# Two blocks of a model on one core: the tiles that are loaded as stationary operands get start addresses that are multiples of 128 bytes

## The chip, the core and the metric

The kernel runs on one core of a Trainium2 chip. The time is device microseconds of one execution, the median of several. TensorE does the matrix products: for each one it first loads a stationary operand (the "weights" of the array, an instruction of its own, LDWEIGHTS) and then streams a moving operand past it (MATMUL). In the rows below, `d<-ws,h` is a matmul that writes the PSUM tile `d` from the moving tile `ws` and the stationary tile `h`: the last name is the stationary one.

## The reference, cut to what matters

Two blocks follow each other on 2048 tokens of width 1024, all in float32.

```python
# first block
p = rmsnorm(x) @ w_in                       # pool mixer, 4 differential heads, 4 stick-breaking heads
x = x + concat(pool, diff_attention, stick_breaking) @ w_out
x = x + (silu(rmsnorm(x) @ w_gate) * (rmsnorm(x) @ w_up)) @ w_down      # width 2816
x = rmsnorm(x)
# second block
proj = modulated_rmsnorm(x) @ w_in_2        # 7 parts of 512: gated spatial branch and retention branch
y = concat(gmlp_branch, retention_branch) @ w_out_2
out = x + gate * rmsnorm(y)
```

## The kernel before

Tokens go through in four blocks of 512. Every large product is exact to float32 by splitting both operands into a high and a low part (`float32r`, one pass each): `mm3` issues three matmuls for each 128 rows of the contraction, hi*hi, hi*lo and lo*hi, at lines 149, 150 and 151. `dense_T` takes the model's weights `ws` as stationary operand and streams the activations; `dense_N` takes a 128x128 piece of the activations as stationary operand and streams 512 columns of `ws`.

Phase 1 runs the projection of a block (activations `h`) beside the attention of the block before (queries `q` stationary with keys `k` moving at line 557; for the stick-breaking heads values `v` stationary with `pT` moving at line 709; for the differential heads `pT` stationary), and then the output projections (activations `h`, and in the last one the first four of the eight 128-row pieces in tiles `s`). Phase 2 is the feed-forward: gate and up products by `dense_T` (`d` and `u`), then the down product by `dense_N` with stationary tiles `a`. Phase 3 is the second block: seven projections by `dense_N` from `h`, small retention products, and the output projection by `dense_N` with stationary tiles `y`.

The order in which each engine gets its instructions is made at build time by a scheduler that models the engines; nothing is reordered between engines on the chip but by semaphores. Tiles lie in pools, one after another in each partition; a tile starts where the one before ends, at the next multiple of 32 bytes. Pools with narrow tiles (tables of 4, 8 or 16 numbers) therefore push the pools that follow them off the multiples of 128.

The built program gives these places to the stationary operands of nearly all matmuls (bytes past a multiple of 128, in the kernel before and after the change; a piece of a tile is always a multiple of 512 bytes from the tile's start), with the number of their matmuls:

```
stationary      moving (before, now)   matmuls                        before  now
h               ws (0, 0)              3744 of 512, 384 of 256 cols        0    0
ws              h (0, 0)               5568 of 512                         0    0
a               ws (0, 0)              2112 of 512                        32    0
y               ws (0, 0)               768 of 512                        96    0
q               k (64, 96)              672 of 512, 288 narrower          64    0
v (float32r)    pT (96, 96)             224 of 512, 96 narrower           64    0
s, pieces 0, 1  ws (0, 0)                48 of 512                        32   32
s, pieces 2, 3  ws (0, 0)                48 of 512                         0    0
pT (float32)    v (64, 0)               544 of 128                        96   96
x (transposes)  identity (32, 32)       480 of 128                         0   64
b, tmp          several                 508 of 128                        96   64
wsT             b (96, 64)               16 of 512                         0   64
```

Of the kernel before, what the change touches and what calls it, by code (L numbers as in the profile page):

```python
# [17 lines left out]
P = 128  # L18
# [7 lines left out]
NFF = DFF // P  # L26
EPS = 1e-6
NEG = -1.0e30
LARGEST = 3.0e38
# [5 lines left out]
def constants():  # L35
    """Tables that depend on shapes alone."""
    f = np.float32
    c = {}
    c["ident"] = np.eye(P, dtype=f)
    p = np.arange(P)  # L40
    tri = np.where(p[None, :] <= p[:, None], 0.0, NEG).astype(f)
    mask_le = np.concatenate([np.zeros((P, 384), f), tri], axis=1)
    mask_lt = np.where(p[None, :] < p[:, None], 0.0, NEG).astype(f)
    inv_cnt = np.zeros((P, 2, 16), f)
    inv_w = np.zeros((P, 2), f)
    for ch in range(2):
        for half in range(2):
            w = WINDOWS[2 * ch + half]
            rows = slice(64 * half, 64 * half + 64)
            inv_cnt[rows, ch] = (1.0 / np.minimum(np.arange(16) + 1, w)).astype(f)  # L50
            inv_w[rows, ch] = 1.0 / w
    c["tab1"] = np.concatenate([mask_le, inv_cnt.reshape(P, 32), inv_w, mask_lt], axis=1)
    gam = 1.0 - 2.0 ** (-5.0 - np.arange(RH))
    t = np.zeros((P, RH, P))
    for h in range(RH):
        t[:, h] = np.where(p[None, :] >= p[:, None], gam[h] ** -(p[:, None] + 1.0), 0.0)
    c["ret_mask"] = (t * RD ** -0.5).astype(f)
    c["ret_kdec"] = np.stack([gam[h] ** (P - 1.0 - p) * RD ** -0.5 for h in range(RH)], 1).astype(f)
    c["ret_qdec"] = np.stack([gam[h] ** (p + 1.0) for h in range(RH)], 1).astype(f)
    c["ret_qdec2"] = np.stack([gam[h] ** (2 * (p + 1.0)) for h in range(RH)], 1).astype(f)  # L60
    half = RD // 2
    e = (np.arange(half, dtype=f) / f(half)).astype(f)
    inv_freq = (f(1.0) / np.power(f(10000.0), e).astype(f)).astype(f)
    c["inv_freq"] = np.ascontiguousarray(np.broadcast_to(inv_freq, (P, half)))
    c["gmlp_causal"] = (p[:, None] >= p[None, :]).astype(f)
    return c


def layouts(inputs):
    """Small inputs laid out for the chip: vectors as columns, the four pool matrices as diagonal blocks."""  # L70
    cols = lambda v: v.reshape(-1, P).T
# [25 lines left out]

PROJ_NS, OUT_NS = 107.5e3, 44.4e3       # tensor-engine time of one block's projections


class Body:
# [9 lines left out]
    def t(self, pool, shape, tag, dt=F32, bufs=None):  # L111
        kw = {} if bufs is None else {"bufs": bufs}
        return pool.tile(shape, dt, tag=tag, name=self.nm(tag), **kw)

    def hp(self, kind="e"):
        return self.tc.high_priority(self.pri[kind])

# [1 line left out]
    def split(self, hi, lo, src):  # L119
        """src = hi + lo exactly, both in the single-pass format."""  # L120
        nc = self.nc
# [3 lines left out]
    def wgroup(self, w, k0, nk, c0, ncols):  # L125
        """Weights w[128*k0 : 128*(k0+nk), c0 : c0+ncols], split; get(kc, hl, lo, n)."""
        nc = self.nc
# [17 lines left out]
    def mm3(self, ps, pairs):  # L145
        """ps = sum of products of split operands: hi*hi + hi*lo + lo*hi."""
        n = len(pairs)
# [6 lines left out]
    def dense_T(self, ps, get, c, act):  # L154
        """ps[cols, tokens] = w[:, cols]^T act^T."""
        return self.mm3(ps, [((lambda hl, k=k: get(k, hl, c, P)), (lambda hl, k=k: act[k][:, hl]))
                      for k in range(len(act))])

    def dense_N(self, ps, get, n, act, t):
        """ps[tokens of chunk t, cols] = act w[:, cols]."""  # L160
        return self.mm3(ps, [((lambda hl, k=k: act[k][:, hl, t * P:(t + 1) * P]),
                       (lambda hl, k=k: get(k, hl, 0, n))) for k in range(len(act))])

    def rsqrt_mean(self, ss, n, mul, pool=None):
        """(ss * mul + EPS) ** -0.5 on [P, n]."""
        nc = self.nc
# [15 lines left out]
    def transposed(self, xs, evac, banks, spare=None):  # L182
        """Tiles of act^T (split) for four natural token tiles xs; banks: (PSUM pool, tag) in turn."""
        nc = self.nc
# [21 lines left out]
    def normed(self, src):  # L206
        """Natural tiles of rmsnorm(src) without its gain; src(t) gives a DRAM AP [128, D]."""
        nc = self.nc
# [11 lines left out]
    def normed_first(self, src):  # L220
        """As normed, the tiles one by one and on both engines: nothing else can run yet."""
        nc = self.nc
# [29 lines left out]
    def cols(self, v):  # L252
        """A vector [n] as columns [128, n/128]."""
        return v.rearrange("(k p) -> p k", p=P)

# [1 line left out]
    def run(self):  # L257
        tc, nc, a = self.tc, self.nc, self.a
        with ExitStack() as es:
# [9 lines left out]
            self.raw_bufs, self.ws_bufs = 2, 5  # L269
            # how many steps ahead of their place weights, splits, evacuations and scores are scheduled  # L270
            self.pri = dict(w=100, x=0, e=300, s=20)
# [26 lines left out]

# [1 line left out]
    def phase1(self):  # L300
# [45 lines left out]
    def paced(self, steps):  # L346
        """Emit steps (each yields its tensor-engine ns); the time before each and its last matmul."""
        marks, ns = [], 0.0
# [5 lines left out]
    def spread(self, steps, total, paced):  # L354
        """Emit steps that fill the gaps of the paced ones, held back to an even share of them."""
        marks, ns = paced
# [12 lines left out]
    def attention(self, b):  # L369
        """Scores of a unit are issued one unit ahead of its value products."""  # L370
        units = []
# [17 lines left out]
    def lambda_col(self):  # L389
        """-lambda on every partition."""  # L390
        nc, a = self.nc, self.a
# [156 lines left out]
    def scores(self, q, ks, c, k0, w, extra=False):  # L548
        """[128 queries of chunk c, w keys from k0]: exact in hi and lo parts."""
        nc = self.nc  # L550
# [95 lines left out]
    def head_norm(self, src, width, r1, dst):  # L646
        """Headwise norm (its gain is applied to mix^T) of the query chunks from c0 on, one for each of dst."""
        nc = self.nc
# [18 lines left out]
    def sb_unit(self, b, hh, kb, head):  # L667
        """One stick-breaking head, one block of 512 keys; the blocks are swept from the right."""
        nc = self.nc
# [110 lines left out]

# [1 line left out]
    def phase2(self):  # L782
# [58 lines left out]

# [1 line left out]
    def prepare3(self):  # L843
        """Per-channel vectors, modulation, rotary tables and masked spatial weights."""
        nc, a, c3 = self.nc, self.a, self.c3
# [15 lines left out]
        nc.vector.memset(ones, 1.0)  # L861
        # modulation
        nc.scalar.activation(cc, cc, AF.Silu)
# [28 lines left out]
        nc.vector.scalar_tensor_tensor(out=self.gpre, in0=self.gpre, scalar=1.0, in1=gp, op0=ALU.add, op1=ALU.mult)  # L892
        # masked spatial weights, transposed
        causal = self.const("gmlp_causal", [P, P], a["gmlp_causal"], pool=self.ppool)
# [7 lines left out]
        nc.scalar.activation(self.wsT.rearrange("p g t -> p (g t)"), ps, AF.Copy)  # L902
        # rotary tables
        nt = S // P
        posi = self.const("positions_2", [P, nt], a["positions_2"][0].rearrange("(t p) -> p t", p=P), dt=I32, pool=c3)
        pos = c3.tile([P, nt], F32, name="pos")
        nc.vector.tensor_copy(pos, posi)
        fr = self.const("inv_freq", [P, 64], a["inv_freq"], pool=c3)
        halfpi = c3.tile([P, 1], F32, name="halfpi")
# [32 lines left out]
    def group_stats(self, parts, name):  # L942
        """Mean and variance along each of the four parts: tile [P, 4, 2]."""
        nc = self.nc
# [35 lines left out]
    def second(self, b):  # L980
# [11 lines left out]
        act = []  # L992
        # gated spatial branch
        vn = self.t(self.bpool, [P, 4, NT, P], "b")
# [36 lines left out]
        if b < NB - 1:  # L1031
            xs_next = self.second_in(b + 1)
        # retention branch
        kr = self.t(self.bpool, [P, NT, RH, RD], "b")
# [83 lines left out]
        def use_rg(t, ps):  # L1118
            s_ = self.t(self.tpool, [P, 512], "rg")
            nc.scalar.activation(s_, ps, AF.Silu)  # L1120
            nc.vector.tensor_tensor(out=yy[:, t], in0=yy[:, t], in1=s_, op=ALU.mult)
        # held back, to fill the waits of the last chunks
        project(3072, use_rg, [marks[i] for i in (6, 7, 9, 10)])
        to_act(yy)
        if b < NB - 1:
            self.h_next = drain(self.second_T(xs_next))
        # output projection
        yb = [self.t(self.bpool, [P, 2, D], "b") for _ in range(2)]
# [50 lines left out]
```

## Time and profile before

| | |
|---|---|
| median of 3 runs | 3684.72 us (3682.74 to 3689.01) |
| profiled execution, first to last instruction (span) | 3681.9 us |
| TensorE matmul busy | 3591.9 us, 98% of the span, 17664 records |
| TensorE weight load busy | 2982.3 us, 81% |
| VectorE, ScalarE, GpSimd busy | 54%, 40%, 13% |
| mean granted TensorE clock | 0.995 |

The profile records one execution. Its own time is its span; the median of the runs lies 2.8 us above it, the fastest run 0.8 us. A float32 product that isn't split shows as two matmul records, so there are more records than matmuls in the program. The duration given for a matmul overlaps the next one's; how fast they follow each other is read from their starts.

### The profile page before, as it was taken

Reading aid. Unit: us, or ns where it says so; the run is one execution under the profiler, and the core shown is the slowest. Engines: PE = TensorE matmul, PEld = TensorE weight load, DVE = VectorE, ACT = ScalarE, POOL = GpSimd, SP = SyncE. Lnnn points to the kernel's source line nnn. Section 1 sums busy time; section 2 is a strip of 40 time slices with the busy share of each in tenths; the row PEclk is TensorE's granted clock in tenths of the full one; section 3 lists DMA queues with packets and bytes.
Section 4 is the critical chain, followed back from the end, with each engine's and each line's share of the span. In section 5 each row is a group of like instructions: output and inputs, shape, how many; then the busy total and the mean of one; then the engine's idle time right before and its main releaser. Section 6 shows DMA issues by size and latency. Waiting matters only on the chain. (4 is left out here: it accounts for less than half of the span.)

```text
span 3681.9 us, 46663 instructions
## 1 busy us (share of the span) xinstructions
PE 3591.9 (98%) x17664; PEld 2982.3 (81%) x17664; DVE 1986.9 (54%) x3265; ACT 1489.7 (40%) x2588; POOL 466.0 (13%) x769
## 2 busy tenths in 40 slices
PE   8999999989899999999999999999999999999998
PEld 6888888877788888888888888888888878878887
DVE  4557776899866444453334333433345554655444
ACT  4656666676655332233223222322232332333322
POOL 2343231231001100000000000000001120211101
PEclk9999999999999999999999999999999999999999
DMA  7776655644454554443324333433343252432431
GB/s 242 218 213 186 176 172 158 180 126 149 126 159 146 167 171 137 132 159 113 92 92 151 113 92 97 166 115 92 95 145 105 79 178 87 127 118 77 158 91 63
DMA packets 336065, 503.01 MB, mean 137 GB/s; under 512 B 29152, under 2 KB 198112, under 8 KB 335840
## 3 DMA queue, kind: packets, MB, share of 16 engines
q1 hardware_dynamic: 312336, 426.08, 38.2%
q0 software_dynamic: 23504, 73.95, 5.9%
q8 instruction: 139, 2.28, 0.3%
q14 instruction: 86, 0.70, 0.1%
HBM read 424.70 MB, written 75.24 MB: 136 GB/s over the span
## 5 line engine op out<-in xcount | busy, mean ns | idle before, releaser
L123 DVE TENSOR_TENSOR ws<-raw,ws 128x1024 fp32r<-128x1024 f32 x520 | 636.0, 1225 | 630.2 <-ACT ws L122 625.5
L122 ACT ACTIVATE ws<-raw 128x1024 fp32r<-128x1024 f32 x520 | 551.2, 1062 | 959.1 <-PE d L151 527.7
L149 PE MATMUL d<-ws,h 128*128 128x512 f32 (+1 forms) x1376 | 533.9, 390 | 5.0 <-ACT b L1008 4.5
L150 PE MATMUL d<-ws,h 128*128 128x512 f32 (+1 forms) x1376 | 526.1, 383 | 0.0
L151 PE MATMUL d<-ws,h 128*128 128x512 f32 (+1 forms) x1376 | 525.6, 383 | 0.0
L149 PE MATMUL d<-h,ws 128*128 128x512 f32 x1152 | 453.0, 393 | 4.9 <-DVE st L123 4.7
L150 PE MATMUL d<-h,ws 128*128 128x512 f32 x1152 | 450.7, 391 | 0.0
L151 PE MATMUL d<-h,ws 128*128 128x512 f32 x1152 | 450.4, 391 | 0.0
L149 PEld LDWEIGHTS d<-ws,h 128*128 128x128 f32 x1376 | 260.1, 189 | 53.5 <-ACT b L1008 5.8
L151 PEld LDWEIGHTS d<-ws,h 128*128 128x128 f32 x1376 | 259.8, 189 | 48.7
L150 PEld LDWEIGHTS d<-ws,h 128*128 128x128 f32 x1376 | 260.4, 189 | 46.3 <-issue 1.0
L557 PE MATMUL s<-k,q 128*128 128x512 f32 (+2 forms) x960 | 276.6, 388 | 11.1 <-DVE r L664 2.9
L149 PE MATMUL d<-ws,a 128*128 128x512 f32 x704 | 279.0, 398 | 1.6 <-DVE res L837 1.6
L150 PE MATMUL d<-ws,a 128*128 128x512 f32 x704 | 279.4, 398 | 0.0
L151 PE MATMUL d<-ws,a 128*128 128x512 f32 x704 | 276.2, 394 | 0.0
L151 PE MATMUL u<-h,ws 128*128 128x512 f32 x704 | 274.3, 390 | 0.8 <-DVE ws L123 0.8
L149 PE MATMUL u<-h,ws 128*128 128x512 f32 x704 | 274.1, 389 | 0.3 <-ACT ws L122 0.3
L150 PE MATMUL u<-h,ws 128*128 128x512 f32 x704 | 273.9, 389 | 0.0
L149 PEld LDWEIGHTS d<-h,ws 128*128 128x128 f32 x1152 | 216.8, 188 | 49.5 <-DVE st L123 5.1
L151 PEld LDWEIGHTS d<-h,ws 128*128 128x128 f32 x1152 | 216.6, 188 | 44.9
L150 PEld LDWEIGHTS d<-h,ws 128*128 128x128 f32 x1152 | 216.9, 188 | 43.5
L557 PEld LDWEIGHTS s<-k,q 128*128 128x128 f32 x960 | 165.8, 194 | 37.4 <-DVE s L588 5.4
(237 smaller groups left out, 5545.0 us busy)
## 6 DMA issues: line engine op xcount, KB each, us to landing
raw<-in_w_in_dram SPq DMA_DIRECT2D x192, 512.0 KB, 4.1
raw<-in_w_gate_dram SPq DMA_DIRECT2D x88, 512.0 KB, 3.8
raw<-in_w_up_dram SPq DMA_DIRECT2D x88, 512.0 KB, 3.8
raw<-in_w_down_dram SPq DMA_DIRECT2D x88, 512.0 KB, 3.6
raw<-in_w_out_dram SPq DMA_DIRECT2D x64, 512.0 KB, 3.9
k<-qkd SPq DMA_DIRECT2D x120, 256.0 KB, 4.1
qkd<-st POOLq DMA_DIRECT2D x192, 128.0 KB, 3.4
q<-qkd SPq DMA_DIRECT2D x96, 256.0 KB, 4.8
```

The costliest lines, as they stand in the source:

```text
L122: nc.scalar.activation(hi, src, AF.Copy)
L123: nc.vector.tensor_tensor(out=lo, in0=src, in1=hi.bitcast(F32), op=ALU.subtract)
L149: self.nc.tensor.matmul(ps, st(0), mv(0), start=i == 0, stop=False)
L150: self.nc.tensor.matmul(ps, st(0), mv(1), start=False, stop=False)
L151: self.nc.tensor.matmul(ps, st(1), mv(0), start=False, stop=i == n - 1)
L557: nc.tensor.matmul(ps[:, :w], q[:, hl, c * P:(c + 1) * P], kt[:, o:o + w], start=hl == 0, stop=hl == 1 and not extra)
```

## The change

Tiles with the tags `h`, `ws`, `a`, `y`, `q` and `v` are allocated with `align_bytes=128`. Two small tables that only `prepare3` reads, the positions and the inverse frequencies, move from a pool that lives to the end (`c3`) to the pool of that preparation (`ppool`). Comments and docstrings are gone, so lines shift by up to 3. No instruction is added or removed.

```diff
+STATIONARY = {"h", "ws", "a", "y", "q", "v"}
...
     def t(self, pool, shape, tag, dt=F32, bufs=None):
         kw = {} if bufs is None else {"bufs": bufs}
+        if tag in STATIONARY:
+            kw["align_bytes"] = 128
         return pool.tile(shape, dt, tag=tag, name=self.nm(tag), **kw)
...
-        posi = self.const("positions_2", [P, nt], a["positions_2"][0].rearrange("(t p) -> p t", p=P), dt=I32, pool=c3)
+        posi = self.const("positions_2", [P, nt], a["positions_2"][0].rearrange("(t p) -> p t", p=P), dt=I32, pool=self.ppool)
...
-        fr = self.const("inv_freq", [P, 64], a["inv_freq"], pool=c3)
+        fr = self.const("inv_freq", [P, 64], a["inv_freq"], pool=self.ppool)
```

On TensorE, ScalarE and GpSimd every instruction keeps its place. Three instructions move. On SyncE, which issues the loads, the two tables stood before the change behind the last of the small tables, at the end of phase 1, ahead of the last loads of `x` for the output projection:

```order
L246 DMA c_b_ada_cols<-in_b_ada_dram 128x16x1
L246 DMA c_positions_15579<-in_positions_dram 128x16x1
L246 DMA c_inv_freq<-in_inv_freq_dram 128x64
L775 DMA st_12984<-in_x_dram 128x512
L775 DMA st_13013<-in_x_dram 128x512
```

Now they stand 21 loads later, early in phase 2, between two other loads of the preparation and a load of feed-forward weights (`raw`):

```order
L874 DMA px_15460<-in_w_ada_dram 128x1024
L249 DMA c_gmlp_causal<-in_gmlp_causal_dram 128x128
L249 DMA c_positions_15579<-in_positions_dram 128x16x1
L249 DMA c_inv_freq<-in_inv_freq_dram 128x64
L138 DMA raw_13346<-in_w_up_dram 128x4x256
```

On VectorE the conversion of the positions (CAST) stood between two evacuations of the output projection (`st`):

```order
L202 SCALAR_TENSOR_TENSOR h_13132<-tp_13127,c_gains,h_13132 128x512
L778 TENSOR_TENSOR st_12819<-d_12821,st_12819 128x512
L907 CAST pos<-c_positions_15579 128x16
L778 TENSOR_TENSOR st_12848<-d_12850,st_12848 128x512
L202 SCALAR_TENSOR_TENSOR h_13140<-tp_13135,c_gains,h_13140 128x512
```

Now it stands in phase 2, behind the first product of the modulation (`px`) and ahead of a gate product (`sg`) and the scaling of the next block's tokens (`x`):

```order
L126 TENSOR_TENSOR ws_13343<-raw_13341,ws_13343 128x1024
L876 TENSOR_SCALAR px_15459<-px_15460,c_c_15450 128x1024
L910 CAST pos<-c_positions_15579 128x16
L828 TENSOR_TENSOR sg_13325<-sg_13325,u_13300 128x512
L219 TENSOR_SCALAR x_15147<-x_15147,rs_r_15165 128x1024
```

What moved there is the CAST alone; its neighbours follow each other as before.

## Rows read from the trace of the kernel before

**Rows 1.** Page: busy time of the engines; TensorE's granted clock in 40 slices.
```profile
PE 3591.9 (98%) x17664; PEld 2982.3 (81%) x17664; DVE 1986.9 (54%) x3265; ACT 1489.7 (40%) x2588; POOL 466.0 (13%) x769
...
PEclk9999999999999999999999999999999999999999
```
**Rows 2.** Windows of phases 1, 2 and 3: length, busy time and records by engine.
```profile
0.00:1255.00 1255.00, 1188.72 (x6712) 1009.84 (x6713) 896.88 (x1614) 766.26 (x1641) 295.07 (x537) 0.99 0.57 172
1255.00:2752.00 1497.00, 1494.28 (x6611) 1224.76 (x6610) 592.73 (x651) 433.43 (x532) 20.50 (x35) 1.00 0.40 123
2752.00:3682.00 930.00, 908.92 (x4344) 747.74 (x4342) 497.30 (x1000) 290.05 (x416) 150.43 (x197) 1.00 0.35 110
```
**Rows 3.** Longest waits of TensorE in phase 1: total us, times, longest.
```profile
PE o L709 <- DVE pT L123: 17.3, 24, 1.6
```
**Rows 4.** Longest waits of TensorE in phases 2 and 3.
```profile
PE d L149 <- ACT b L1008: 4.5, 3, 2.0
```
**Rows 5.** Windows from a run's first matmul to the next run's first: a, ws, a, y, h.
```profile
1739.17:1783.96 44.79, 44.79 (x193) 36.04 (x192) 14.94 (x17) 7.95 (x8) 0.00 (x0) 1.00 0.25 73
1783.97:1871.04 87.07, 87.07 (x385) 72.09 (x384) 30.28 (x32) 26.46 (x32) 0.00 (x0) 1.00 0.36 108
1871.06:1915.84 44.78, 44.78 (x193) 36.04 (x192) 14.95 (x17) 7.95 (x8) 0.00 (x0) 1.00 0.23 73
2948.39:2982.08 33.69, 33.69 (x144) 27.06 (x145) 15.21 (x16) 11.41 (x20) 4.66 (x9) 1.00 0.61 193
3447.99:3502.38 54.39, 54.39 (x241) 45.06 (x240) 23.72 (x61) 16.10 (x20) 15.12 (x15) 1.00 0.47 148
```
**Rows 6.** TensorE's groups by line and shape: busy us, mean ns; idle before.
```profile
L150 PE MATMUL d<-ws,a 128*128 128x512 f32 x704 | 279.4, 398 | 0.0
...
L557 PE MATMUL s<-k,q 128*128 128x512 f32 x672 | 214.5, 416 | 5.8 <-ACT s L686 2.8 <-DVE s L588 2.2 <-DVE s L602 0.4
...
L150 PE MATMUL d<-ws,y 128*128 128x512 f32 x256 | 101.1, 395 | 0.0
...
L709 PE MATMUL o<-pT,v 128*128 128x512 f32 x224 | 90.0, 439 | 13.4 <-DVE pT L123 10.6 <-ACT pT L122 2.4
...
L1020 PE MATMUL tp<-c_ident,b 128*128 128x128 f32 x128 | 19.4, 274 | 0.4 <-DVE b L1121 0.4
L190 PE MATMUL pp<-c_ident,x 128*128 128x128 f32 x128 | 19.3, 273 | 0.0
```
**Rows 7.** TensorE's timeline in attention: start us, us, instruction and count.
```profile
702.50 0.62 PE L557 MATMUL s<-k,q 128*128 128x512 f32 x2
702.96 0.39 PE L150 MATMUL d<-h,ws 128*128 128x512 f32 x1
...
718.30 0.63 PE L709 MATMUL o<-pT,v 128*128 128x512 f32 x2
718.77 0.38 PE L716 MATMUL tp<-c_ident,s 128*128 128x128 f32 x2
```
**Rows 8.** TensorE's timeline in the last output projection; three rows left out each time.
```profile
1234.76 0.39 PE L149 MATMUL d<-ws,s 128*128 128x512 f32 x1
...
1235.69 0.40 PE L150 MATMUL d<-ws,s 128*128 128x512 f32 x1
...
1236.85 0.39 PE L151 MATMUL d<-ws,s 128*128 128x512 f32 x1
...
1237.76 0.39 PE L149 MATMUL d<-ws,h 128*128 128x512 f32 x1
```
**Rows 9.** Timelines of VectorE and SyncE around the three moved instructions.
```profile
1242.65 0.17 DVE L907 CAST pos<-c_positions 128x16 f32<-128x16 int32 x1 [5.60 <-DMA c_positions<-in_positions_dram]
...
1287.66 0.33 SPq L246 DMA_DIRECT2D c_gmlp_causal<-in_gmlp_causal_dram  x1
1292.88 0.38 SPq L135 DMA_DIRECT2D raw<-in_w_up_dram  x1
...
1297.84 0.75 DVE L873 TENSOR_SCALAR px<-px,c_c 128x1024 f32<-128x1024 f32 x1 [0.35 <-DMA px<-in_w_ada_dram]
```

## The prediction

> **What bounds the kernel now.** I read the page's head first: TensorE is busy 98% of the span and no other engine over 54%, at the full clock throughout (the 2.4 GHz level) [rows 1]. The windows by phase say where that is not quite so: in phase 1 TensorE's rows leave 66 us of 1255 uncovered, in phase 2 only 3 of 1497, in phase 3 21 of 930 [rows 2]. The waits name no single cause: the longest sum in phase 1 is 17 us, for the split of `pT` on VectorE [rows 3], the longest behind it 4.5 us [rows 4]. So in phase 2 nearly every nanosecond between two matmuls' starts is time of the kernel, in phase 3 most, in phase 1 a good part. The change moves addresses, so the question is whether the distance from start to start of two matmuls depends on the stationary tile's address.
>
> The trace can answer that, since some stationary tiles begin at a multiple of 128 bytes already. I took stretches in which TensorE does one thing without a gap and divided their length by the matmuls that start in them (a window's count is one higher where the tail of the matmul ahead reaches in). All are of 512 columns, with the moving operand at a multiple of 128 [rows 5]:
> - `a` stationary, 32 bytes off: 44.79 / 192 = 233.3 ns, and again 44.78 / 192;
> - `ws` stationary, at a multiple: 87.07 / 384 = 226.7 ns, between those two stretches;
> - `y` stationary, 96 off: 33.69 / 144 = 234.0 ns;
> - `h` stationary, at a multiple: 54.39 / 240 = 226.6 ns.
>
> The last two have the same code and the same moving tiles, so it isn't the form of the product. It could still be where in the memory the tiles lie. The last output projection speaks against it: its tiles `s` lie side by side, the first two pieces 32 off, the other two at a multiple. From 1234.76 to 1235.69 four matmuls start with 32-off pieces, 0.93 us or 232 ns each; from 1236.85 to 1237.76 four with pieces at a multiple, 0.91 us or 227 ns [rows 8]. A difference of 20 ns read at 10 ns is weak by itself, but it falls on the same side as the other four.
>
> **The change, part by part.** Clock and order on TensorE stay.
>
> *`a`, the down product.* 704 matmuls on each of three lines, 2112 [rows 6], each 233.3 - 226.7 = 6.6 ns shorter: 13.9 us, all in phase 2, where TensorE waits for almost nothing. The feed holds: the stretch of 44.79 us has 14.94 us of VectorE and 7.95 us of ScalarE in it [rows 5], so a stretch of 43.5 us has room.
>
> *`y`, the second output projection.* 256 on each line, 768 [rows 6], at 234.0 - 226.6 = 7.4 ns: 5.7 us. The stretch of 144 has 15.21 us of VectorE in 33.69 [rows 5]; covered as well.
>
> *`q` and `v`, attention.* 672 and 224 matmuls of 512 columns [rows 6], and 384 narrower ones by the table of places. Their mean durations of 416 and 439 ns contain waits and don't serve [rows 6]. The timeline gives pairs without one: 702.50 to 702.96 is 230 ns each for `q`, 718.30 to 718.77 is 235 ns each for `v` [rows 7]. Against 226.7 that is 3 to 8 ns. With 5 ns for all 1280 the sum is 6.4 us; TensorE stands idle 66 us in this phase [rows 2], and where it waits for a `pT` the shorter matmul only makes it wait longer. I take 4 us. The lower end is 0; the upper end is 8.3 ns on all 1280, 10.6 us.
>
> *`h` and `ws`* were at multiples and stay there: 0.
>
> *Tiles that shift along.* `x` goes from 0 to 64 as the stationary operand of 480 transposes. Transposes of `x` at 0 have 273 ns, those of `b` at 96 have 274 [rows 6]: 1 ns on 480 is under 0.5 us, I take 0. `wsT` goes from 0 to 64 for 16 matmuls; at 7 ns and two records each that is 0.2 us. `k`, which `q` meets as moving operand, goes from 64 to 96: see the third rival.
>
> *The three moved instructions.* Before, the CAST held VectorE 5.60 us until its load came, with an evacuation behind it [rows 9]; TensorE lost at most the waits of phase 1 there, and I take 0. Now the two loads are issued between 1287.66 and 1292.88, where SyncE issued nothing for 4.9 us [rows 9]. The CAST stands behind the `px` product that ends at 1298.59 [rows 9], 10.6 us after the issue; the split of later weights stands behind it. If the load has come by then the price is 0, and that is what I take; the bound above is the wait it had before, 5.6 us, if all of it reached TensorE.
>
> *Sum.* 13.9 + 5.7 + 4 = 23.6 us less than the profiled 3681.9, so a span near 3658. The median of the runs lay 2.8 us above the span; 3684.7 - 23.6 = 3661.
>
> *A rule that speaks against it.* The trace has 233 to 234 ns off the multiples of 128 and 227 at them [rows 5]. The Trainium skill, "SBUF — State Buffer", section "Specifications (TRN2)", counts in lines of 16 bytes: an access pays when it crosses to a new line. 32, 64 and 96 bytes off are whole lines, so by that page a tile touches as many lines after the change as before and the sum would be 0, at 3684.7. The rows speak against that as the whole story. The same page's section "Operand start alignment" asks only for a multiple of the element's size and says that its runs timed nothing.
>
> **The rivals.**
>
> *1. Nothing comes of it.* The 6 to 7 ns belong to something that goes with the place, not with the multiple (`a` and `y` both lie high in the memory, `h` and `ws` low). Then the down stretch stays at 44.8 us and the time at 3685. For it: two of my three comparisons are between distant tiles. Against it: the neighbours in [rows 8], and 7 ns on both `a` and `y`, which other code fills. 0.04. By the page's lines of 16 bytes it would end here too, and the trace doesn't agree.
>
> *2. More comes of it.* Matmuls of `h` and `ws` mixed with those of `q` and `v` in phase 1 may pay for their neighbours; then the attention's part reaches its upper end or beyond, and the time is 3684.7 - 13.9 - 5.7 - 10.6 = 3654.5 or less. For it: [rows 7] has an `h` product directly behind each pair. Against it: the idle time of that phase. 0.08.
>
> *3. Part is given back by the moving side.* `v` pairs have `pT` 96 off and take 235 ns, `q` pairs have `k` 64 off and take 230 [rows 7]. If it is the moving operand that makes the 5 ns, `k` at 96 gives 672 x 5 = 3.4 us, or 960 x 5 = 4.8 us, back, and `q` and `v` gain nothing: 3684.7 - 13.9 - 5.7 + 4.8 = 3670. Against it: one pair of each is little to build on. 0.08.
>
> *4. Slower.* The CAST is on VectorE's path in order. If the load of the positions comes late in the traffic at the start of phase 2, the splits behind the CAST wait, then the stationary tiles, then TensorE. It decides once TensorE stands longer than the 23.6 us that the matmuls give: with the CAST ready at 1298.59, the load would have to land 10.6 + 23.6 = 34 us after its issue. At 42 us, say, TensorE would stand 31 us and the time would be 3692. The wait it had before, 5.60 us, is far below that [rows 9]. 0.02.
>
> **How the numbers follow.** The forecast has 0.78: 3661 us. The likeliest value is 3655 to 3668; with the unknown of attention (0 to 10.6) and the third rival the range is 3654 to 3671. Under 0.2% (7.4 us) a measurement of this kernel can hardly tell from no change. Forecast, second and third rival all lie beyond it on the fast side: 0.78 + 0.08 + 0.08 = 0.94 faster; 0.04 the same; 0.02 slower.
>
> **What would show it.** The stretch of 192 `a` matmuls should take 43.5 us, that of 144 `y` matmuls 32.6 us, while the 384 of `ws` keep 87.1 us. Phase 2 should shrink by 14 us, phase 3 by 5 to 6, phase 1 by 0 to 10. The durations of `d<-ws,a` and `d<-ws,y` should fall from 395 to 398 ns to those of `h` at its best, and VectorE should not wait at the CAST. I am wrong if `a` stays at 233 ns (the multiple of 128 isn't the cause), if phase 2 shrinks by much less than 14 us while the stretch is at 43.5 (a new wait), or if phase 1 grows.

## The result and the profile after

The changed kernel takes 3727.26 us (median of four runs, 3725.41 to 3731.84) where the kernel before takes 3683.73 us (3681.86 to 3689.01) beside it: a ratio of 1.0119, with an interval of 1.0105 to 1.0134. It is slower by 43.5 us, or 1.2%. The forecast was 3661 us, and faster.

The head of its page: the granted clock is 0.995 as before, and TensorE has as many records; its busy time and the span have grown together, by 46.6 and 43.4 us against [rows 1] and the span of before.

```profile
span 3725.3 us, 46660 instructions
...
PE 3638.5 (98%) x17664; PEld 2988.4 (80%) x17664; DVE 1992.3 (53%) x3265; ACT 1489.3 (40%) x2588; POOL 457.0 (12%) x769
```

The same five stretches as in [rows 5], of `a`, `ws`, `a`, `y` and `h` as stationary operand, in the windows of the changed kernel (start and end, length, then busy time and records of TensorE, its weight loads, VectorE, ScalarE and GpSimd, granted clock, DMA share and GB/s):

```profile
1755.71:1800.49 44.78, 44.78 (x193) 36.04 (x192) 15.04 (x17) 7.94 (x8) 0.00 (x0) 1.00 0.23 74
1800.50:1890.09 89.59, 89.59 (x385) 72.10 (x384) 30.14 (x32) 26.44 (x32) 0.00 (x0) 1.00 0.33 104
1890.10:1934.88 44.78, 44.78 (x193) 36.04 (x192) 15.39 (x17) 7.94 (x8) 0.00 (x0) 1.00 0.22 74
2985.76:3019.44 33.68, 33.68 (x144) 27.10 (x145) 15.20 (x16) 11.14 (x19) 4.65 (x9) 1.00 0.60 196
3487.97:3543.72 55.75, 55.75 (x241) 45.23 (x240) 23.55 (x61) 16.09 (x20) 13.28 (x15) 1.00 0.44 146
```

Divided by their matmuls (192, 384, 192, 144 and 240), these are 233.2, 233.3, 233.2, 233.9 and 232.3 ns. `a` and `y` have gained nothing, though they now lie at multiples of 128. `ws` and `h`, which were to stay as they were, have lost: 87.07 us became 89.59, and 54.39 became 55.75.

Where the time went, in windows whose borders are the first gate or up product and the last down product: first the kernel before, then the changed one.

```profile
0.00:1278.67 1278.67, 1212.39 (x6821) 1029.35 (x6822) 907.24 (x1626) 773.95 (x1650) 297.23 (x541) 0.99 0.57 172
1278.67:2751.46 1472.79, 1470.07 (x6500) 1204.81 (x6498) 582.37 (x639) 425.20 (x524) 18.34 (x31) 1.00 0.39 123
2751.46:3681.90 930.44, 909.46 (x4346) 748.19 (x4344) 497.30 (x1000) 290.59 (x417) 150.43 (x197) 1.00 0.35 110
```
```profile
0.00:1288.09 1288.09, 1223.04 (x6822) 1033.14 (x6822) 908.53 (x1626) 774.22 (x1650) 297.33 (x541) 0.99 0.56 170
1288.09:2785.19 1497.10, 1495.01 (x6500) 1206.22 (x6499) 584.98 (x640) 424.09 (x521) 18.24 (x31) 1.00 0.37 121
2785.19:3725.30 940.11, 920.50 (x4346) 749.07 (x4344) 498.79 (x1000) 290.95 (x418) 141.43 (x197) 1.00 0.34 109
```

Phase 1 is 9.4 us longer, phase 2 24.3, phase 3 9.7. In each it is TensorE's busy time that grew, not what it leaves uncovered (65 us in phase 1 now, 66 before; 2.1 and 2.7 in phase 2; 19.6 and 21.0 in phase 3). Nor is there a new wait. The longest of TensorE's waits behind phase 1 in the changed kernel (engine, line, what ended the wait: total us, times, longest):

```profile
PE d L152 <- DVE res L840: 1.4, 1, 1.4
...
PE d L152 <- DVE b L1143: 3.8, 4, 1.3
```

And the CAST, whose load was the fourth rival, waits 0.20 us. VectorE's timeline around it in the changed kernel, which answers to [rows 9]:

```profile
1306.61 0.75 DVE L876 TENSOR_SCALAR px<-px,c_c 128x1024 f32<-128x1024 f32 x1 [0.48 <-DMA px<-in_w_ada_dram]
1307.56 0.17 DVE L910 CAST pos<-c_positions 128x16 f32<-128x16 int32 x1 [0.20 <-DMA c_positions<-in_positions_dram]
```

So the loss is a few nanoseconds on each of some nine thousand matmuls, with nothing waiting. The mean durations, which overlap, show it less clearly than the starts. On the middle line of `mm3`, `ws` as stationary operand goes from 391 to 396 ns (first the kernel before, then the changed one), `a` from 398 in [rows 6] to 396, and `y` stays at 395.

```profile
L150 PE MATMUL d<-h,ws 128*128 128x512 f32 x1152 | 450.7, 391 | 0.0
```
```profile
L153 PE MATMUL d<-h,ws 128*128 128x512 f32 x1152 | 456.2, 396 | 0.0
...
L153 PE MATMUL d<-ws,a 128*128 128x512 f32 x704 | 277.9, 396 | 0.0
...
L153 PE MATMUL d<-ws,y 128*128 128x512 f32 x256 | 101.1, 395 | 0.0
```

What had moved is told by the places in the built programs, now counted to 256 instead of 128 (bytes past a multiple; the pairs that were equal are marked):

```
stationary / moving   before        after        
ws / h                0 / 0   =     0 / 128
h / ws                0 / 0   =     128 / 0
a / ws                160 / 0       128 / 0
y / ws                224 / 0       128 / 0
q / k                 192 / 192 =   128 / 224
v / pT                192 / 224     0 / 96
```

`h` was at a multiple of 128 before and after, but it moved, from byte 66304 to 66432: the pool of `ws` ahead of it is now an aligned pool, and 128 bytes of slack behind it push everything that follows. In the table ahead of the prediction, which counts to 128, this can't be seen.

### The profile page after: what moved, and what is told of

Read it like the earlier page. It is cut to its first block, busy times and chain, and to the rows that moved or that the text cites. A ratio compares the mean times of both kernels' runs of the same rounds, so it can differ in the third digit from the quotient of the medians.

```text
span 3725.3 us, 46660 instructions
## 1 busy us (share of the span) xinstructions
PE 3638.5 (98%) x17664; PEld 2988.4 (80%) x17664; DVE 1992.3 (53%) x3265; ACT 1489.3 (40%) x2588; POOL 457.0 (12%) x769
## 5 line engine op out<-in xcount | busy, mean ns | idle before, releaser
L152 PE MATMUL d<-h,ws 128*128 128x512 f32 x1152 | 458.4, 398 | 4.4 <-DVE st L126 4.2
L153 PE MATMUL d<-h,ws 128*128 128x512 f32 x1152 | 456.2, 396 | 0.0
L154 PE MATMUL d<-h,ws 128*128 128x512 f32 x1152 | 456.1, 396 | 0.0
L152 PE MATMUL u<-h,ws 128*128 128x512 f32 x704 | 278.2, 395 | 0.4 <-ACT ws L125 0.4
L154 PE MATMUL u<-h,ws 128*128 128x512 f32 x704 | 278.2, 395 | 0.3 <-DVE ws L126 0.3
L153 PE MATMUL u<-h,ws 128*128 128x512 f32 x704 | 278.1, 395 | 0.0
L828 DVE TENSOR_TENSOR sg<-sg,u 128x512 f32<-128x512 f32 x88 | 60.5, 688 | 265.6 <-PE u L154 258.7
```

Source lines behind the costliest of these rows:

```text
L152: self.nc.tensor.matmul(ps, st(0), mv(0), start=i == 0, stop=False)
L153: self.nc.tensor.matmul(ps, st(0), mv(1), start=False, stop=False)
L154: self.nc.tensor.matmul(ps, st(1), mv(0), start=False, stop=i == n - 1)
L828: nc.vector.tensor_tensor(out=sg, in0=sg, in1=pu, op=ALU.mult)
```

## The experiments

Three theories stood at the start. A: the start of each operand by itself matters, at a multiple of 256 and not of 128. B: the distance from the stationary to the moving operand's start matters, modulo 256. C: the time belongs to something other than addresses. Before the change `ws` lay at 0, so A and B gave the same for all its products, and there was no tile 128 off by which 128 and 256 differ.

**micro_starts: the disputed cost by itself.** Two large tiles in memory, nothing of the model; blocks of 48 matmuls in the order of `mm3`, with 512 moving columns, whose pieces start a chosen number of bytes past a multiple of 1024. It was executed once; each pair of starts has two blocks in it.

```diff
+PAIRS = [(0, 0), ..., (32, 0), (64, 0), (96, 0), (128, 0), ..., (0, 64), ..., (0, 128), ..., (32, 32), ..., (128, 128), ..., (128, 384), ...]
...
+    S0 = lambda k, hl: st[:, so + 1024 * (k % 4) + 512 * hl:so + 1024 * (k % 4) + 512 * hl + P]
+    M0 = lambda k, hl: mv[:, mo + 2048 * (k % 4) + 1024 * hl:mo + 2048 * (k % 4) + 1024 * hl + TB]
```

> This kernel does none of the model: it times matmuls by themselves. In blocks of 48 (hi*hi, hi*lo, lo*hi over 16 pieces, as the kernel's own products, 512 columns, split format) it sets the start of the stationary and of the moving operand to chosen numbers of bytes past a multiple of 1024, 31 pairs, each twice. Theory A (each operand's own start must be a multiple of 256): a block takes 226.7 ns per matmul where both starts are multiples of 256, and 232 to 234 in every other pair, the pairs with equal offsets such as 128 and 128 among them. Theory B (the distance of the two starts must be a multiple of 256): equal offsets (32 and 32, 64 and 64, 128 and 128, 192 and 192, 128 and 384) take 226.7 too, and 233 where they differ. Theory C (it isn't addresses at all, but where the program's instructions or other tiles fell): all pairs take the same.

Windows from a block's first matmul to the next block's, with (stationary, moving) at (0, 0), (32, 0), (128, 0), (0, 64), (0, 128), (32, 32), (128, 128) and (128, 384):

```profile
66.40:77.29 10.89, 10.89 (x50) 9.01 (x48) 0.00 (x0) 0.60 (x1) 0.00 (x0) 1.00 0.01 2
77.29:88.48 11.19, 11.19 (x50) 9.02 (x48) 0.00 (x0) 0.60 (x1) 0.00 (x0) 1.00 0.00 0
110.92:122.07 11.15, 11.15 (x49) 9.04 (x48) 0.00 (x0) 0.60 (x1) 0.00 (x0) 1.00 0.00 0
188.43:199.43 11.00, 11.00 (x50) 9.01 (x48) 0.00 (x0) 0.60 (x1) 0.00 (x0) 1.00 0.00 0
210.64:221.84 11.20, 11.20 (x50) 9.01 (x48) 0.00 (x0) 0.60 (x1) 0.00 (x0) 1.00 0.01 1
243.94:254.86 10.92, 10.92 (x50) 9.02 (x49) 0.00 (x0) 0.60 (x1) 0.00 (x0) 1.00 0.01 2
265.76:276.68 10.92, 10.92 (x49) 9.01 (x48) 0.00 (x0) 0.60 (x1) 0.00 (x0) 1.00 0.01 2
309.73:320.63 10.90, 10.90 (x50) 9.01 (x48) 0.00 (x0) 0.60 (x1) 0.00 (x0) 1.00 0.00 0
```

By 48 these are 226.9, 233.1, 232.3, 229.2, 233.3, 227.5, 227.5 and 227.1 ns. Both operands 32 off, or both 128 off, cost nothing; one of them 32 or 128 off costs 5 to 6 ns, the moving one 64 off 2 ns; a distance of exactly 256 counts as none. A falls by (128, 128) and (32, 32), C by all of it, and B holds. All the pairs that are equal modulo 256 had 226.7 to 227.6 inside their blocks. The unequal ones had 232 to 234, with three exceptions: 229 where the moving operand lies 64 bytes past the stationary one, modulo 256; 226.8 in one block and 233.3 in the other at (16, 0); and 231.6 at (0, 16). Clock, loads and streams are the same in all rows.

**e_pad256: all distances 0 in the kernel.** The changed kernel without alignment, but with pads that put `ws`, `h`, `a`, `y`, `q`, `k`, `v` and `pT` all at 0 past a multiple of 256 (`s` isn't).

```diff
-        if tag in STATIONARY:
-            kw["align_bytes"] = 128
+    def pad(self, pool, nbytes):
+        pool.tile([P, nbytes // 4], F32, tag="pad", name=self.nm("pad"), bufs=1)
...
+            self.pad(self.small, 64)
...
+            self.pad(pool("pad_e"), 224)
             self.epool = pool("ev", bufs=5)
...
+            self.pad(pool("pad_a"), 96)
             self.apool = pool("act", bufs=10)
...
+            self.pad(self.tiny, 32)
             self.ypool = pool("y3", bufs=8)
```

> The changed kernel with the alignment taken out and four pads of 32 to 224 bytes put in, so that h, ws, a, y, q, k, v and pT all start at multiples of 256 bytes. Theories A and B both give 226.7 ns for the stretches of ws, h, a and y: against the kernel before 13.9 us for a, 5.7 for y, 0 to 10 in attention, so about 3661 us (3654 to 3666), ratio to before 0.994. Theory C (the moved tables or the place of the program make every matmul 6.5 ns longer): 3720 to 3727 as the changed kernel.

3662.17 us (3660.62 to 3673.22), ratio 0.9946, interval 0.9924 to 0.9967: faster than both kernels. The stretches of `a`, `ws`, `y` and `h`:

```profile
1739.53:1783.03 43.50, 43.50 (x193) 36.04 (x192) 15.36 (x17) 7.95 (x8) 0.00 (x0) 1.00 0.25 75
1783.05:1870.07 87.02, 87.02 (x385) 72.09 (x384) 30.16 (x32) 26.34 (x32) 0.00 (x0) 1.00 0.36 108
2941.15:2973.96 32.81, 32.81 (x144) 27.07 (x145) 15.21 (x16) 10.79 (x19) 4.70 (x9) 1.00 0.60 196
3438.43:3492.82 54.39, 54.39 (x241) 45.06 (x240) 23.85 (x62) 16.09 (x20) 15.05 (x15) 1.00 0.48 151
```

43.50 us for `a` is the number that the prediction had written for the change. It took another distance to get it.

The medians make the gain too large, because three of this kernel's four runs had a higher mean granted clock than most of those beside it. At 0.993 its one run took 3673.22 us, and eleven runs of the kernel before 3681.55 to 3691.32 (median 3686.67); at 0.996 to 0.997 it took 3660.62 to 3662.84, and the kernel before 3674.04 to 3675.97. Both comparisons give 13 us, not 23. That the median falls next to the 3661 of the prediction and of the expectation is in part luck.

**e_h_back: `h` left where it was.** Two tags out of the set, so that no slack comes ahead of `h`; `y` ends at a multiple of 256, `a` 128 off, `q`/`k` 0/32, `v`/`pT` 128/160.

```diff
-STATIONARY = {"h", "ws", "a", "y", "q", "v"}
+STATIONARY = {"a", "y", "q", "v"}
```

> The changed kernel with the tags h and ws left out of the set that is aligned: by the built program h is at a multiple of 256 again (as before the change), as are ws, q and y; a is 128 past one, k 32 past one. Theories A and B: stretches of ws and h at 226.7 ns again, y at 226.7 as well (0 off, where the changed kernel has 128 and 232 to 233), a stays at 233. Time: before less 5.7 for y, so 3678, with attention 3672 to 3684. Theory C: about 3727, with ws and h at 233.

3680.9 us (3673.74 to 3685.57), ratio 0.9985, interval 0.9974 to 0.9996. The stretches of `a`, `ws` and `y`:

```profile
1740.66:1785.27 44.61, 44.61 (x193) 36.18 (x192) 15.32 (x17) 7.95 (x8) 0.00 (x0) 1.00 0.25 75
1785.29:1872.32 87.03, 87.03 (x385) 72.06 (x384) 30.28 (x32) 26.34 (x32) 0.00 (x0) 1.00 0.36 108
3183.42:3216.23 32.81, 32.81 (x144) 27.07 (x145) 15.21 (x16) 10.91 (x19) 4.67 (x9) 1.00 0.59 195
```

`ws` is back at 226.6 ns, `y` has its gain, and `a`, aligned to 128 and 128 off its partner, still takes 232.3. The whole loss is gone, and the time lies where it was expected.

**e_tables: the moved tables alone.** The set of tags is gone, the rest of the change stands.

```diff
-        if tag in STATIONARY:
-            kw["align_bytes"] = 128
```

> The other part of the change alone: the two tables in the preparation's pool, no alignment at all. Places past a multiple of 256: h and ws 0 as before, a 96 (before 160), y 160 (before 224), q and k 192 as before. Theories A and B: the time of the kernel before, 3684, within 3 us. Theory C: slower, up to 3727.

3687.12 us (3677.18 to 3689.77), ratio 1.0006, interval 0.9993 to 1.002. The three moved instructions cost nothing that can be measured beside the kernel before (3685.19 us).

**e_h_off: the loss without the alignment.** The moved tables, no alignment, and one pad of 128 bytes ahead of the pool of `h`.

```diff
-        if tag in STATIONARY:
-            kw["align_bytes"] = 128
...
+            self.pad(pool("pad_h"), 128)
             self.hpool = pool("h", bufs=8)
```

> The kernel with the moved tables and no alignment (as e_tables), with one pad of 128 bytes ahead of the pool of h: h lies 128 past a multiple of 256 while ws stays at 0; a, y, q, v and their partners stay unequal, as before. Theory B (the distance of the two starts, modulo 256): stretches of ws and of h at 233 ns instead of 226.7, time 3720 to 3730, as the changed kernel, without any alignment in it. Theory A (each start by itself) gives the same here. If the changed kernel's loss came from its align_bytes in another way, this one stays at 3687.

3731.75 us (3728.77 to 3732.38), ratio 1.0131, interval 1.0116 to 1.0146. The stretches of `a` and `ws`:

```profile
1759.10:1803.88 44.78, 44.78 (x193) 35.99 (x192) 14.98 (x17) 7.94 (x8) 0.00 (x0) 1.00 0.25 73
1803.90:1893.47 89.57, 89.57 (x385) 72.08 (x384) 30.12 (x32) 26.47 (x32) 0.00 (x0) 1.00 0.35 105
```

That is the changed kernel's 89.59 us for `ws`, and its whole loss, from 128 bytes ahead of `h`; the time is 1.8 us over the expected range. All pools behind `h` move along, but `a` and `y` stay unequal to `ws` (224 and 32 past a multiple of 256). `q` and `k` both lie at 64, so they are equal, as they were before the change, and not unequal as the expectation says.

**e_ws_out: the changed kernel with one word less.** Without the slack behind `ws`, `h` goes back, and the alignments that remain happen to put `a` and `y` at 0; `q`/`k` are 128/128, `v`/`pT` 128/0.

```diff
-STATIONARY = {"h", "ws", "a", "y", "q", "v"}
+STATIONARY = {"h", "a", "y", "q", "v"}
```

> The changed kernel with one tag, ws, taken out of the set. ws itself starts at the same place without it; the pool behind it no longer gets slack of 128 bytes, and all later pools move down: past a multiple of 256 h, a, y and ws lie at 0, q and k both at 128, v at 128 with pT at 0. Theory B: 226.7 ns for ws, h, a and y, q and k equal too, v alone unequal: 3662 to 3667. If the pads as such or their number mattered, not the distances, it stays at the changed kernel's 3727.

3671.87 us (3664.13 to 3673.58), ratio 0.9966, interval 0.9954 to 0.9978. The stretches of `a` and `ws`:

```profile
1738.40:1781.90 43.50, 43.50 (x193) 36.04 (x192) 15.36 (x17) 7.95 (x8) 0.00 (x0) 1.00 0.24 76
1781.92:1868.95 87.03, 87.03 (x385) 72.07 (x384) 30.26 (x32) 26.34 (x32) 0.00 (x0) 1.00 0.37 108
```

One name in the set of tags turns 1.2% slower into 0.3% faster. The expected 3662 to 3667 us were missed by 5; the kernel before, beside it, took 3682.57.

**e_shift128: every start 128 off, every distance 0.** The pads of e_pad256 and one of 128 bytes ahead of everything, which is the sharpest test of A against B in the kernel itself.

```diff
+            self.pad(self.cpool, 128)
             self.wpool = pool("w")
```

> As e_pad256, with a further pad of 128 bytes ahead of everything: ws, h, a, y, q, k, v and pT all lie 128 past a multiple of 256, so no start is at a multiple of 256 and all distances are 0. Theory B: 226.7 ns in all stretches, time as e_pad256, 3662 within 5. Theory A: 233 in all stretches, 3727 or more.

3669.26 us (3663.4 to 3670.85), ratio 0.9958, interval 0.9942 to 0.9975. `a` and `ws` once more:

```profile
1738.36:1781.86 43.50, 43.50 (x193) 36.03 (x192) 15.25 (x17) 7.95 (x8) 0.00 (x0) 1.00 0.27 76
1781.88:1868.90 87.02, 87.02 (x385) 72.07 (x384) 29.43 (x32) 26.35 (x32) 0.00 (x0) 1.00 0.36 107
```

None of the eight kinds of tiles that e_pad256 had put at a multiple of 256 lies at one here, and `a` and `ws` take as little as in any run. The time is 2.3 us over the expected 3662 within 5; the kernel before, beside it, took 3682.57, so the gain is 13 us, that of e_pad256 at an equal clock.

**micro_turns: which load against which stream, and how far the cost goes.** The blocks of micro_starts, with pairs in turns from matmul to matmul, finer distances, fewer columns and plain float32. B1 takes the distance of a matmul's own two operands, B2 that of the next load to the stream under way. Each block is a list of pairs in turn, the columns, and 1 for plain float32. It was executed once.

```diff
+BLOCKS = [..., ([(0, 128)], 512, 0), ([(0, 0), (128, 128)], 512, 0), ([(0, 128), (128, 0)], 512, 0), ..., ([(0, 0)], 384, 0), ([(0, 128)], 384, 0), ..., ([(0, 0)], 512, 1), ...]
```

> Matmuls by themselves again, none of the model. First, blocks in which the matmuls take two pairs of starts in turn (stationary, moving, bytes past a multiple of 1024). If what counts is the distance within a matmul (theory B1), turns of (0, 0) and (128, 128) take 226.7 ns per matmul and turns of (0, 128) and (128, 0) take 232 to 234. If the load of the next stationary tile meets the moving tile that is being streamed (theory B2), it is the other way round: turns of (0, 0) and (128, 128) take 232 to 234, turns of (0, 128) and (128, 0) take 226.7; turns of (0, 0) and (0, 128), and of (0, 0) and (128, 0), lie between. Second, finer distances: 226.7 near 0 (4, 8 or 16 bytes), about 229 near 64 and 232 to 234 elsewhere, if the pattern of the first such kernel holds. Third, fewer columns: the same 6 to 7 ns at 384 columns if it is a cost per load of a stationary tile, 5 at 384 and 3 at 256 if it goes with the columns streamed; and plain float32, where the changed kernel's transposes and products showed no difference: the same time for all pairs.

Blocks of (0, 128); of turns (0, 0)/(128, 128); of turns (0, 128)/(128, 0); of turns (0, 0)/(128, 0); of (0, 4); then 384 columns at (0, 0) and (0, 128); 256 columns at (0, 0) and (0, 128); plain float32 with 512 columns at (0, 0) and (0, 128), where a matmul is two records:

```profile
85.65:96.84 11.19, 11.19 (x49) 9.01 (x48) 0.00 (x0) 0.60 (x1) 0.00 (x0) 1.00 0.00 0
96.84:107.80 10.96, 10.96 (x49) 9.00 (x48) 0.00 (x0) 0.60 (x1) 0.00 (x0) 1.00 0.01 1
107.80:118.85 11.05, 11.05 (x50) 9.03 (x49) 0.00 (x0) 0.60 (x1) 0.00 (x0) 1.00 0.00 0
129.89:141.03 11.14, 11.14 (x49) 9.01 (x48) 0.00 (x0) 0.60 (x1) 0.00 (x0) 1.00 0.01 1
141.03:152.38 11.35, 11.35 (x49) 9.01 (x48) 0.00 (x0) 0.60 (x1) 0.00 (x0) 1.00 0.00 0
264.04:272.36 8.32, 8.32 (x50) 8.32 (x48) 0.00 (x0) 0.60 (x1) 0.00 (x0) 1.00 0.00 0
272.36:280.81 8.45, 8.45 (x50) 8.45 (x49) 0.00 (x0) 0.49 (x1) 0.00 (x0) 1.00 0.01 2
297.57:303.33 5.76, 5.76 (x50) 5.76 (x50) 0.00 (x0) 0.49 (x1) 0.00 (x0) 1.00 0.01 3
303.33:309.03 5.70, 5.70 (x51) 5.70 (x49) 0.00 (x0) 0.39 (x1) 0.00 (x0) 1.00 0.00 0
341.76:383.02 41.26, 41.26 (x99) 18.30 (x99) 0.00 (x0) 0.28 (x1) 0.00 (x0) 1.00 0.00 0
383.02:424.22 41.20, 41.20 (x98) 18.24 (x97) 0.00 (x0) 0.60 (x1) 0.00 (x0) 1.00 0.00 0
```

Turns cost 228.3 ns with equal pairs and 230.2 with unequal ones: between 226.9 and 233.1 both, so neither B1 nor B2 is clean, and which of the two it is stays open. Nor do turns of (0, 0) with one unequal pair lie midway in both cases: they took 230.2 with (0, 128) and 232.1 with (128, 0).

With 384 columns the distance costs 2.7 ns (173.3 and 176.0), with 256 nothing (120.0 and 118.8). That is neither the same 6 to 7 ns at 384 nor the 5 and 3 ns that had been expected for a cost by load or by column. In plain float32 it costs nothing (429.8 and 429.2 a record), as expected.

Small distances other than 0 aren't cheap, against what had been expected: 236.5 ns at 4 bytes, 233.6 at 8 and 231.6 at 16. Nor is there a wide dip around 64: 48 took 233.3 and 80 took 231.1. The other distances tried, from 112 to 248 bytes, lie between 230 and 235.

## Why the prediction was wrong

**The step that failed** is "*`h` and `ws`* were at multiples and stay there: 0", and under it the premise that what counts is whether the stationary tile starts at a multiple of 128. The quantity is the distance of the two starts, and its modulus is 256. The largest group of matmuls, 5568 with `ws` and 3744 with `h` stationary, lost its distance of 0 by `h` moving 128 bytes; e_h_off has the loss with that move and without the alignment.

**How the stretches give the sum:** 5568 x (233.3 - 226.7) = 36.7 us and 3744 x (232.3 - 226.6) = 21.3 us, 58 in all, against 43.5 measured. The two traces tell where the difference is. Counted from each matmul's start to the next one's, over the whole trace, `ws` takes 29.0 us more, `h` 11.7 more, `a` 1.1 and `y` 0.3 less, and all other matmuls 4.3 more, which makes 43.6. (The others take 4.2 us more in e_tables too, which lost nothing, so theirs may be chance.) The mean gap from start to start between two matmuls of one kind, without those of 260 ns and more, which hold waits, is in ns:

```
stationary / moving     before   after
ws / h, phase 1         228.6    232.4
ws / h, phase 2         226.8    233.2
h / ws, phase 1         229.1    232.5
h / ws, phase 3         227.5    232.6
a / ws                  233.4    232.9
y / ws                  233.2    232.6
```

So outside pure stretches the price is smaller: 3.8 ns for `ws` in phase 1, 5.1 and 3.4 for `h`. The rest was taken from waits: what the longer gaps hold beyond the usual one falls from 14.3 to 12.2 us for `ws` and from 23.5 to 18.7 for `h`. Why the price is smaller there isn't shown; the turns of micro_turns show only that neighbours count.

**`a`, 13.9 us, and `y`, 5.7 us:** nothing to speak of in the change, since both came to lie 128 off `ws`, and the prediction's own test ("I am wrong if `a` stays at 233 ns") decided it. At a distance of 0 the gain is there: in e_pad256 the stretches fall to 226.6 and 227.8 ns, so by them the terms are 2112 x (233.3 - 226.6) = 14.2 and 768 x (234.0 - 227.8) = 4.8 us. Counted from start to start over that trace, `a` takes 11.1 and `y` 3.5 us less (10.3 to 13.0 and 3.3 to 3.8 in the three kernels with both at a distance of 0): the longer gaps among those of `a` take 2 us back, and not all of `y` runs as in its stretch. The condition was wrong, and the sizes were 1 to 4 and 2 us too large.

**`q` and `v`, 4 us:** `q` and `k` were equal before, so the 230 ns in [rows 7] were no price of their addresses. The traces bear it out. The gaps without a wait between two `q` matmuls of 512 columns, some 240 in each, have a mean of 230.4 to 231.6 ns in all six kernels where `q` and `k` are equal, at 0, 64, 128 or 192 (231.3 before), and of 233.1 in the changed kernel and 232.8 in e_h_back, where they are not. So there was nothing to gain at `q`, and the change took 1.8 ns there. For `v` there are some 30 such gaps in a trace, too few to tell. At an equal clock e_pad256 gains 13 us, which is no more than `a` and `y` make in its trace.

**Moved tiles and moved instructions, 0:** right; e_tables has 1.0006, and the CAST waits 0.20 us.

**The rivals.** The first ("nothing") is closest in what it said of `a` and `y`, for another reason: the 6 to 7 ns don't go with the place either. The second needed a gain at `q`, and there was a small loss. The third asked about the moving side and had the right kind of question; it put it to `q` and `v` alone, not to `ws` and `h`, which trade sides. The fourth, the only slower one, didn't happen. A rival that moved `h` was missing, though the order of the pools and the byte 66304 could be read from the built program.

**Why the evidence fooled.** In the five stretches and the `s` pieces the moving operand lay at 0 and the slow tiles 32, 160 or 224 off. These fit "multiple of 128", "multiple of 256" and "distance" alike. Only a tile 128 off, or a moving operand off 0, could have told them apart, and the `q` pairs, with both at 192, were the one such place; their 230 ns were read as 3 ns of price, where equal starts in six kernels take as much.

**The rule that was weighed.** By the 16-byte lines of the Trainium skill, "SBUF — State Buffer", section "Specifications (TRN2)", a start 32 or 128 bytes off costs nothing. The trace agrees for both operands moved together (227.5 ns) and disagrees for one alone (233.1 and 232.3). The Trainium skill, "SBUF — State Buffer", section "Who interferes with whom", gives TensorE two independent read ports, one for the moving operand and one for the weight load. The runs have one load and one stream in all blocks, and 226.9 or 233.3 ns by the distance of their addresses alone; so at 512 and at 384 columns (173.3 or 176.0) the time depends on the two addresses together, and the trace doesn't agree with reads that are without effect on each other. At 256 columns (120.0 and 118.8 ns) the trace shows nothing against it. What inside the memory makes this is not shown by any run.

## What to carry to other kernels

Where TensorE is busy nearly all the time with 512-column split matmuls and a weight load for each, put the stationary and the moving tile at the same place modulo 256 bytes, and check each pair in the built addresses, with how many matmuls it has; an alignment of each tile by itself says nothing of the pair. An alignment request also moves all the pools behind it, so before it is costed at nothing for tiles that "are aligned already", their addresses before and after must be compared. Compare such kernels at the same mean granted clock: beside e_pad256, runs of one kernel at 0.996 to 0.997 were some 12 us shorter than those at 0.993, which is as much as the gain. When a few nanoseconds are traced to an address, a small kernel that moves one operand, the other, and both tells in one run what a large one can't.

## What the runs showed of the hardware

- The distance of 256 bytes was not expected: 226.7 to 227.6 ns where both starts are equal modulo 256, 230 to 236.5 elsewhere, 229 with the moving operand 64 past the stationary one, and one block of two at (16, 0) with 226.8. Why 64 is cheaper than 32, 48, 80 or 128 is open.
- The price vanishes at 256 columns and in plain float32, and is 2.7 ns at 384 columns. In those blocks of 384 and 256 columns the weight loads' busy time fills the window as the matmuls' does (8.32 of 8.32 us); at 512 columns it is 9.01 of 10.89. Whether the price comes from that slack between loads was not tried; at 384 columns, where there is none, 2.7 ns are left.
- Runs of one kernel lie up to 17.7 us apart (3674.04 to 3691.70 in nineteen runs of the kernel before), more than `a` gains, with the mean granted clock between 0.992 (the longest) and 0.997. The stretches are steadier: 43.50 us in each of three kernels with `a` at a distance of 0, 87.02 to 87.07 for `ws` in each of five, so the readings rest on them.
